# Up projections of a feed-forward by seven products of quarters, with down projections between them

## The chip, the cores and the metric

The kernel runs on one core of a Trainium2 chip. The metric is the device time of one execution in microseconds; lower is better. The kernel before takes 2473.8 us (median of 3 runs, 2471.67 to 2475.36).

## The reference, cut to what matters

Three layers work on 512 tokens of width 1024. Two are hybrid layers with attention, convolution, retention and a feed-forward; the third has a feed-forward, a mixer and a second feed-forward. The change touches the two feed-forwards of the third layer:

```python
def swiglu_ffn(x, w_in, w_down):
    a, b = jnp.split(x @ w_in, 2, axis=-1)
    return (jax.nn.silu(a) * b) @ w_down
...
    x = x + 0.5 * swiglu_ffn(rmsnorm(x, ffn1_norm), ffn1_w_in, ffn1_w_down)
```

`w_in` is 1024 x 5632, so a and b have 2816 columns each, which is 22 blocks of 128; `w_down` is 2816 x 1024. All data are float32.

## The kernel before

Activations lie transposed: 8 tiles of 128 features x 512 tokens. A float32 product is made from three passes of TensorE. Weights and activations are each split into a rounded high part and the rest (`wh`, `wl`; ScalarE copies, VectorE subtracts), and high x high, low x high and high x low are added in PSUM (`mm3`). One output block of an up projection is 8 blocks of k x 3 = 24 matmuls of 128x128 weights against 512 tokens.

`ffn` works in four chunks of 6, 6, 5 and 5 of the 22 blocks (`CH2`). For a chunk it makes the blocks of a and b in turn (`gemm`, `e_up`: times `rb`, the norm's scale for each token; Silu for a; a x b; split into `hid`), and then the eight output blocks of the down projection over this chunk's `hid` (6 or 5 blocks of k x 3 matmuls each), each added to `x` by VectorE (`e_dn`). `wload` loads a weight tile (`raw`, 512 KB) and splits it. The last four down blocks of the second feed-forward run in two halves of 256 tokens (`tail`).

The order of all work is made by a planner. Every call is recorded with its reads and writes (`record`). `order` then gives each engine its list: it steps through an estimated time, starts what can start first, and among those that could start within 20 ns takes the one recorded first. `ahead(n)` makes a piece of work count as recorded n instructions earlier (`AHEAD` = 400 for weights and evictions). `emit` issues everything in the planned order from one line (475), which is why all rows below have that line. Tiles come from pools with a fixed number of buffers: 80 work tiles `t` (`NT`), 3 `raw` (`NR`), 4 `wh` and 4 `wl` (`NW`), 8 PSUM tiles `p` of one bank each (512 float32 a partition).

In `record` an operation depends on those that touched the same columns; and for a tile of a pool, in the order of recording:

```python
op.deps.add(a[-1] if w and eng == "PE" else t[1])
```

`a[-1]` is the last recorded access of this tile, any columns; `t[1]` is the first one. So TensorE's write depends on the last access, all others on the first.

Of the kernel before, what the change touches and what calls it, by code (L numbers as in the profile page):

```python
# [10 lines left out]
F32 = mybir.dt.float32  # L11
F32R = mybir.dt.float32r
AF = mybir.ActivationFunctionType
OP = mybir.AluOpType
AX = mybir.AxisListType

P = 128
S = 512
NB = S // P
D = 1024  # L20
KT = D // P
# [83 lines left out]
CH2 = [(0, 6), (6, 12), (12, 17), (17, 22)]  # L105
FF2 = 22
# [82 lines left out]
class _Engine:  # L189


    def __init__(self, plan, name, real):
        self._plan, self._name, self._real = plan, name, real
# [7 lines left out]
class Plan:  # L201
# [96 lines left out]
    @staticmethod  # L298
    def _cost(eng, method, args, kw, writes, reads):
        out = writes[0]  # L300
        n = 1
        for _, c in out.ap[1:]:
            n *= c

        def psum(x):
            return "PSUM" in str(x.space)

        table = 0
        if eng == "PE":
            if method == "transpose":  # L310
                return 2 * n / 2.4 + 1, 0
            m = reads[0].ap[-1][1] if len(reads[0].ap) == 2 else P
            load = 18 + .695 * m
            if reads[0].dtype == F32:
                return max(4 * n / 2.4, 2 * load) + 3, 0
            return max(n / 2.4, load) + 3, 0
        if eng == "ACT":
            f = kw.get("func", args[2] if len(args) > 2 else None)
            table = Plan.TABLES.get(str(f).split(".")[-1], 0)
            return .833 * n + (51 if psum(reads[0]) else 94) + (187 if "accum_out" in kw else 0), table  # L320
        if eng == "DVE":
            ptr = 60 if n > 8 and any(x.ap[-1][1] == 1 and len(x.ap) == 2 for x in reads) else 0
            if method == "reciprocal":
                return 62 + 8.3 * n, 0
            if method == "tensor_reduce":
                n = 1
                for _, c in reads[0].ap[1:]:
                    n *= c
            fast = method in ("tensor_scalar", "tensor_copy", "memset") and not any(map(psum, writes + reads))
            return 68 + ptr + (.52 if fast else 1.042) * n, 0  # L330
        if eng == "POOL" and method != "dma_start":
            return 80 + (2.3 if method == "tensor_tensor" else 1.28 if method == "affine_select" else 1.0) * n, 0
        b = 4
        for _, c in out.ap:
            b *= c
        run = min(4 * x.ap[-1][1] if x.ap[-1][0] == 1 else 4 for x in writes + reads)
        return b / 360.0 * max(1.0, 512.0 / run), 0


    def order(self):  # L340
# [153 lines left out]
class Net:  # L494
    def __init__(self, ctx, tc, d, where):
        self.tc, self.d, self.where = tc, d, where
        self.nc = self.plan = Plan(tc.nc)
        self.const = ctx.enter_context(tc.tile_pool(name="const", bufs=1))
        self.wp = ctx.enter_context(tc.tile_pool(name="wp", bufs=1))
        self.sb = ctx.enter_context(tc.tile_pool(name="sb", bufs=1))  # L500
        self.dr = ctx.enter_context(tc.tile_pool(name="dr", bufs=1, space=bass.MemoryType.DRAM))
        self.ps = ctx.enter_context(tc.tile_pool(name="ps", bufs=1, space=bass.MemoryType.PSUM))
        self.NT = 80
        self.NR, self.NW = 3, 4
        self.AHEAD = 400
        self.LATER = 300
        self.WAIT = 52
        self.mr = self.px = None
        self.STAT = 40
        self.PARK = 300  # L510
        self.ORDER = "card"
        self.PC, self.PA, self.PR = 4, 1, 1
        self.SHIFT = 10
        self.EARLY = 60
# [142 lines left out]
    def gemm(self, srcs, acts, evict, wide=4, bg=None, steps=0, per=1, both=False):  # L657


        n = len(acts)  # L660
        i = 0
        first = True
        while i < len(srcs):
            g = srcs[i:i + (wide if first else 1)]
            first = False
            with self.plan.ahead(self.AHEAD):
                ws = [self.wload(s, n * P * per) for s in g]
            pss = [[self.psg() for _ in range(per)] for _ in g]
            for k in range(n):
                for (h, l), pp in zip(ws, pss):  # L670
                    for j, ps in enumerate(pp):
                        s = slice((j * n + k) * P, (j * n + k + 1) * P)
                        self.mm3(ps, (h[:, s], l[:, s]), acts[k], k == 0, k == n - 1)
            with self.plan.ahead(self.AHEAD):
                for j, pp in enumerate(pss):
                    evict(i + j, *pp)
            i += len(g)
            if bg:
                if both:
                    self.pump_all(bg)  # L680
                else:
                    self.pump(bg, steps)


    def rsqrt(self, v, n):
# [1069 lines left out]
                    nc.sync.dma_start(out[k][:, s], x)  # L1755

    def ffn(self, n, h=None, out=None):
        nc, d = self.nc, self.d
        h = h or self.hsplit(self.x, f"ffn{n}_norm_2")
        with self.plan.ahead(-self.STAT):  # L1760
            rb = self.rms_r(self.x)
        wi, wd = d[f"f{n}_in"], d[f"f{n}_down"]
        at = 0
        for c, (lo, hi) in enumerate(CH2):
            hid = []
            gate = []

            def e_up(i, ps):
                t = self.T()
                nc.vector.tensor_tensor(t, ps, rb, op=OP.mult)  # L1770
                if i % 2 == 0:
                    nc.scalar.activation(t, t, AF.Silu)
                    gate.append(t)
                else:
                    nc.vector.tensor_tensor(t, t, gate.pop(), op=OP.mult)
                    hid.append(self.split(t))

            srcs = [wi[i + s * FF2] for i in range(lo, hi) for s in range(2)]
            self.gemm(srcs, h, e_up, 4 if c == 0 else 1)

            def e_dn(i, ps):
                nc.vector.scalar_tensor_tensor(self.x[i], ps, 0.5, self.x[i], op0=OP.mult, op1=OP.add)

            m = P * (hi - lo) * P
            down = [wd[at + i * m:at + (i + 1) * m].rearrange("(p f) -> p f", p=P) for i in range(KT)]
            if out is None or hi < FF2:
                self.gemm(down, hid, e_dn, 1)
            else:
                self.gemm(down[:KT - TAIL], hid, e_dn, 1)
                self.tail(down[KT - TAIL:], hid, out)  # L1790
            at += KT * m
# [164 lines left out]
```

## Time and profile before

| | |
|---|---|
| runs | 2473.8, 2471.67, 2475.36 us |
| profiled execution | 2473.95 us, span 2472.2 us |
| instructions | 30175, of them 11506 matmuls |
| mean granted clock of TensorE | 0.993 |
| HBM read, written | 244.54 MB, 22.04 MB |

The span runs from the first to the last instruction. TensorE's matmuls are shown as PE, its weight loads as PEld, VectorE as DVE, ScalarE as ACT, GpSimd as POOL and SyncE, which issues most transfers, as SP. Matmuls are pipelined, so the duration of one is longer than the distance from its start to the next one's. In the first feed-forward of the third layer the chunks follow each other from about 1258.5 to 1617.6 us, up projections and down projections in turn; the second one runs from about 2120 us to the end.

### The profile page before, as it was taken

The numbers are of one execution on the slowest core, as the hardware profiler recorded it, in microseconds if no ns is written. First come the engines' busy times: TensorE is split into PE (matmuls) and PEld (weight loads), VectorE is DVE, ScalarE is ACT, GpSimd is POOL, SyncE is SP. The second block draws the span as 40 slices with busy tenths as digits, with TensorE's granted clock in tenths as the row PEclk, the third lists the DMA queues.
The fourth block names the chain that finished last, engine by engine and source line by source line (L and its number), as shares of the span: only waits on it lengthen the run. The fifth ranks groups of instructions, "written<-read, shape, count | busy, mean of one in ns | idle before, by whom it ended". The sixth has DMA issues, their size and how long they took to land. (4 is left out here: it accounts for less than half of the span.)

```text
span 2472.2 us, 30175 instructions
## 1 busy us (share of the span) xinstructions
PE 2430.0 (98%) x11506; PEld 2017.0 (82%) x11506; DVE 1464.3 (59%) x2529; ACT 949.2 (38%) x1487; POOL 115.2 (5%) x222
## 2 busy tenths in 40 slices
PE   8999999999998999999999999999999999999998
PEld 7878888888887788788888888888888888888887
DVE  7986834545997689744574444556445455444445
ACT  4467422223347643242342222333455334322222
POOL 0011000000001102300000000000000000000000
PEclk9999999999999999999999999999999999999999
DMA  6552333324454334453323233375222243232232
GB/s 211 160 139 95 112 95 101 96 94 129 135 155 122 117 105 148 136 180 94 119 80 96 90 104 98 102 245 164 90 79 70 75 138 109 84 111 88 90 108 67
DMA packets 104785, 286.12 MB, mean 116 GB/s; under 512 B 14272, under 2 KB 21120, under 8 KB 104640
## 3 DMA queue, kind: packets, MB, share of 16 engines
q1 hardware_dynamic: 99808, 270.79, 35.7%
q0 software_dynamic: 4832, 13.41, 1.8%
q8 instruction: 90, 1.47, 0.2%
q14 instruction: 55, 0.45, 0.1%
HBM read 244.54 MB, written 22.04 MB: 108 GB/s over the span
## 5 line engine op out<-in xcount | busy, mean ns | idle before, releaser
L475 PE MATMUL p<-t,wh 128*128 128x512 f32 (+1 forms) x6408 | 1995.6, 390 | 12.7 <-ACT wh L475 7.5
L475 PEld LDWEIGHTS p<-t,wh 128*128 128x128 f32 x6408 | 1203.7, 189 | 261.6 <-ACT wh L475 9.3
L475 PE MATMUL p<-t,wl 128*128 128x512 f32 x3204 | 1249.7, 390 | 1.2 <-DVE wl L475 1.1
L475 ACT ACTIVATE wh<-raw 128x1024 fp32r<-128x1024 f32 (+4 forms) x428 | 426.1, 1000 | 1181.8 <-PE p L475 790.5
L475 PEld LDWEIGHTS p<-t,wl 128*128 128x128 f32 x3204 | 604.2, 189 | 125.4 <-DVE wl L475 3.6
L475 DVE TENSOR_TENSOR wl<-raw,wh 128x1024 fp32r<-128x1024 f32 (+4 forms) x428 | 491.3, 1151 | 146.7 <-ACT wh L475 142.4
L475 DVE TENSOR_TENSOR t<-p,t 128x512 f32<-128x512 f32 (+5 forms) x388 | 237.0, 629 | 449.3 <-PE p L475 441.0
L475 DVE TENSOR_TENSOR t<-t 128x512 f32<-128x512 f32 (+9 forms) x688 | 361.5, 552 | 45.8 <-ACT t L475 35.7
L475 ACT ACTIVATE t<-t 128x512 f32<-128x512 f32 (+3 forms) x409 | 246.9, 617 | 147.0 <-DVE t L475 129.0
L475 PE MATMUL p<-t 128*128 128x256 f32 (+10 forms) x1184 | 181.5, 294 | 11.9 <-DVE t L475 9.2
L475 PEld LDWEIGHTS p<-t 128*128 128x128 f32 (+2 forms) x1184 | 148.9, 173 | 38.8 <-DVE t L475 15.7
L475 DVE TENSOR_TENSOR t<-t,p 128x512 f32<-128x512 f32 x104 | 71.7, 692 | 173.6 <-PE p L475 169.3
L475 ACT ACTIVATE t<-p 128x512 f32<-128x512 f32 (+7 forms) x290 | 129.9, 500 | 75.6 <-PE p L475 67.6
L475 DVE SCALAR_TENSOR_TENSOR t<-t,cols 128x512 fp32r<-128x512 f32 (+32 forms) x196 | 133.9, 717 | 8.8 <-ACT t L475 8.7
L475 DVE SCALAR_TENSOR_TENSOR t<-p,t 128x512 f32<-128x512 f32 (+1 forms) x84 | 57.5, 684 | 125.2 <-PE p L475 125.2
L475 ACT ACTIVATE t<-t,cols 128x512 fp32r<-128x512 f32 (+2 forms) x76 | 49.5, 671 | 29.4 <-DVE t L475 28.7
L475 PE MATMUL p<-ident,t 128*128 128x128 f32 x388 | 55.1, 278 | 5.0 <-DVE t L475 2.7
L475 ACT ACT_TABLE_LOAD x42 | 53.9, 1283 | 11.8 <-DMA t<-in_x 4.0
L475 PEld LDWEIGHTS p<-ident,t 128*128 128x128 f32 x388 | 45.8, 142 | 12.8 <-DVE t L475 4.0
L475 ACT ACTIVATE t<-t,s 128x128 f32<-128x128 f32 (+2 forms) x80 | 42.3, 531 | 15.2 <-DVE s L475 14.6
L475 DVE SCALAR_TENSOR_TENSOR t<-t 128x512 f32<-128x512 f32 (+1 forms) x72 | 44.9, 631 | 1.5
L475 DVE CUSTOM_DVE_ANT_0 t<-p,t 128x256 f32<-128x256 f32 (+2 forms) x80 | 34.5, 450 | 9.4 <-PE p L475 9.1
(58 smaller groups left out, 366.2 us busy)
## 6 DMA issues: line engine op xcount, KB each, us to landing
raw<-in_w_in SPq DMA_DIRECT2D x100, 512.0 KB, 3.8
raw<-in_f_in SPq DMA_DIRECT2D x88, 512.0 KB, 3.5
raw<-in_w_up SPq DMA_DIRECT2D x64, 512.0 KB, 3.6
raw<-in_w_down SPq DMA_DIRECT2D x64, 512.0 KB, 3.6
t<-t SPq DMA_DIRECT2D x126, 128.0 KB, 3.3
raw<-in_w_out SPq DMA_DIRECT2D x24, 512.0 KB, 3.6
raw<-in_f_down SPq DMA_DIRECT2D x32, 384.0 KB, 3.0
raw<-in_f_down SPq DMA_DIRECT2D x32, 320.0 KB, 2.8
```

The costliest lines, as they stand in the source:

```text
L475: fn(*args, **kw)
```

## The change

From the second chunk on, the two up blocks of one index i (a's and b's weights, 1024 x 128 each) are computed together. The weights of both are seen as a 2 x 2 matrix of quarters (block a or b; lower or upper half of k), the activations as 2 x 2 quarters (half of k; half of the tokens), and the product of the two is made by seven products of quarters and sums in place of eight products.

- `halves7` makes the sums of activation quarters once for a feed-forward, beside the first chunk, and splits them: 16 work tiles that stay.
- `wload7` makes the sums of weight quarters: four loads from SP, two loads from GpSimd that add to what is there (`accum_op`), two sums on VectorE; three tiles are split as `wh` and `wl`, and one sum (s4) in work tiles.
- `prod7` is one product: 4 blocks of k x 3 matmuls of 256 columns.
- `pair7` runs the seven products into three half banks: a and b are the halves of one PSUM tile, c is in another. Between products ScalarE copies a (`p1`) and VectorE makes `p1 + b` (`u2_`), a times `rb`, and `w`; after them come the last sums.
- The down projections of a chunk are no longer run behind its up projections but kept (`later`) and recorded one by one between and within the pairs of the next chunk. Only the last chunk's run behind its ups.
- Work tiles go from 80 to 74, `raw` from 3 to 4, `wh` and `wl` from 4 to 5 each, in the whole kernel; the planner counts an adding transfer twice.

```diff
--- before.py
+++ after.py
@@ -334,7 +334,7 @@
         for _, c in out.ap:
             b *= c
         run = min(4 * x.ap[-1][1] if x.ap[-1][0] == 1 else 4 for x in writes + reads)
-        return b / 360.0 * max(1.0, 512.0 / run), 0
+        return b / 360.0 * max(1.0, 512.0 / run) * (2 if kw.get("accum_op") else 1), 0
 
 
     def order(self):
@@ -500,8 +500,8 @@
         self.sb = ctx.enter_context(tc.tile_pool(name="sb", bufs=1))
         self.dr = ctx.enter_context(tc.tile_pool(name="dr", bufs=1, space=bass.MemoryType.DRAM))
         self.ps = ctx.enter_context(tc.tile_pool(name="ps", bufs=1, space=bass.MemoryType.PSUM))
-        self.NT = 80
-        self.NR, self.NW = 3, 4
+        self.NT = 74
+        self.NR, self.NW = 4, 5
         self.AHEAD = 400
         self.LATER = 300
         self.WAIT = 52
@@ -680,6 +680,104 @@
                     self.pump_all(bg)
                 else:
                     self.pump(bg, steps)
+
+
+    def halves7(self, gname):
+
+
+        nc, C = self.nc, S // 2
+        V = nc.vector
+        lo, hi = slice(0, C), slice(C, S)
+        out = []
+        for k in range(KT // 2):
+            a, b = self.T(), self.T()
+            nc.scalar.activation(a, self.x[k], AF.Copy, scale=self.col(gname, k))
+            nc.scalar.activation(b, self.x[k + KT // 2], AF.Copy, scale=self.col(gname, k + KT // 2))
+            q1, q2 = self.T(), self.T()
+            V.tensor_tensor(q1[:, lo], a[:, lo], a[:, hi], op=OP.subtract)
+            V.scalar_tensor_tensor(q1[:, hi], q1[:, lo], -1.0, b[:, hi], op0=OP.mult, op1=OP.subtract)
+            V.tensor_tensor(q2[:, lo], b[:, hi], a[:, hi], op=OP.subtract)
+            V.scalar_tensor_tensor(q2[:, hi], q1[:, hi], -1.0, b[:, lo], op0=OP.mult, op1=OP.subtract)
+            out.append((self.split(q1), self.split(q2)))
+            yield out
+
+    def wload7(self, u1, u2):
+
+        nc = self.nc
+        V = nc.vector
+        n = KT * P
+        lo, hi = slice(0, n // 2), slice(n // 2, n)
+        r1, r2, r3 = (self.plan.pool_tile(self.wp, (P, n), F32, "raw", self.NR) for _ in range(3))
+        nc.sync.dma_start(r1, u1)
+        nc.sync.dma_start(r2[:, lo], u2[:, lo])
+        nc.sync.dma_start(r3[:, lo], u2[:, hi])
+        nc.sync.dma_start(r3[:, hi], u1[:, lo])
+        nc.gpsimd.dma_start(r2[:, lo], u2[:, hi], accum_op=OP.add)
+        nc.gpsimd.dma_start(r3[:, hi], u2[:, lo], accum_op=OP.add)
+        s4 = self.T()
+        V.tensor_tensor(r2[:, hi], r2[:, lo], r1[:, lo], op=OP.add)
+        V.tensor_tensor(s4, r2[:, hi], r1[:, hi], op=OP.add)
+        out = []
+        for r in (r1, r2, r3):
+            h = self.plan.pool_tile(self.wp, (P, n), F32R, "wh", self.NW)
+            l = self.plan.pool_tile(self.wp, (P, n), F32R, "wl", self.NW)
+            nc.scalar.activation(h, r, AF.Copy)
+            V.tensor_tensor(l, r, h.bitcast(F32), op=OP.subtract)
+            out.append(((h[:, lo], l[:, lo]), (h[:, hi], l[:, hi])))
+        (a11, a12), (s1, s2), (a22, s3) = out
+        return a11, a12, a22, s1, s2, s3, self.split(s4)
+
+    def prod7(self, o, w, acts, start):
+
+        mm = self.nc.tensor.matmul
+        wh, wl = w
+        n = len(acts)
+        for k, (ah, al) in enumerate(acts):
+            c = slice(k * P, (k + 1) * P)
+            mm(o, wh[:, c], ah, start=start and k == 0, stop=False, skip_group_check=True)
+            mm(o, wl[:, c], ah, start=False, stop=False, skip_group_check=True)
+            mm(o, wh[:, c], al, start=False, stop=(k == n - 1), skip_group_check=True)
+
+    def pair7(self, u1, u2, h, q):
+
+
+
+        nc, C, K = self.nc, S // 2, KT // 2
+        V = nc.vector
+        lo, hi = slice(0, C), slice(C, S)
+
+        def part(ts, c):
+            return [(x[:, c], y[:, c]) for x, y in ts]
+
+        with self.plan.ahead(self.AHEAD):
+            a11, a12, a22, s1, s2, s3, s4 = self.wload7(u1, u2)
+        q1, q2 = [x for x, _ in q], [y for _, y in q]
+        ab, c = self.psg(), self.psg()[:, lo]
+        a, b = ab[:, lo], ab[:, hi]
+        self.prod7(a, a11, part(h[:K], lo), True)
+        self.prod7(b, s2, part(q1, hi), False)
+        self.prod7(c, s1, part(q1, lo), True)
+        t = self.T()
+        p1, u2_ = t[:, lo], t[:, hi]
+        with self.plan.ahead(self.AHEAD):
+            nc.scalar.activation(p1, a, AF.Copy)
+        self.prod7(a, a12, part(h[K:], lo), False)
+        with self.plan.ahead(self.AHEAD):
+            V.tensor_tensor(u2_, p1, b, op=OP.add)
+        self.prod7(b, s3, part(q2, lo), False)
+        yield None
+        o1, o2 = self.T(), self.T()
+        w = self.T(F32, (P, C))
+        with self.plan.ahead(self.AHEAD):
+            yield a, o1
+            V.tensor_tensor(w, p1, b, op=OP.add)
+            V.tensor_tensor(o2[:, hi], w, c, op=OP.add)
+        self.prod7(b, a22, part(q2, hi), False)
+        self.prod7(c, s4, part(h[K:], hi), False)
+        with self.plan.ahead(self.AHEAD):
+            V.tensor_tensor(o2[:, lo], p1, b, op=OP.add)
+            V.tensor_tensor(o1[:, hi], u2_, c, op=OP.add)
+            yield o1, o2
 
 
     def rsqrt(self, v, n):
@@ -1755,35 +1853,73 @@
                     nc.sync.dma_start(out[k][:, s], x)
 
     def ffn(self, n, h=None, out=None):
+
+
         nc, d = self.nc, self.d
+        V = nc.vector
         h = h or self.hsplit(self.x, f"ffn{n}_norm_2")
         with self.plan.ahead(-self.STAT):
             rb = self.rms_r(self.x)
         wi, wd = d[f"f{n}_in"], d[f"f{n}_down"]
+        C = S // 2
+        lo, hi = slice(0, C), slice(C, S)
         at = 0
-        for c, (lo, hi) in enumerate(CH2):
+        q = []
+
+        def sums():
+            for o in self.halves7(f"ffn{n}_norm_2"):
+                q[:] = o
+                yield
+
+        bg = [sums()]
+        later = []
+        for c, (c0, c1) in enumerate(CH2):
             hid = []
             gate = []
 
             def e_up(i, ps):
                 t = self.T()
-                nc.vector.tensor_tensor(t, ps, rb, op=OP.mult)
+                V.tensor_tensor(t, ps, rb, op=OP.mult)
                 if i % 2 == 0:
                     nc.scalar.activation(t, t, AF.Silu)
                     gate.append(t)
                 else:
-                    nc.vector.tensor_tensor(t, t, gate.pop(), op=OP.mult)
+                    V.tensor_tensor(t, t, gate.pop(), op=OP.mult)
                     hid.append(self.split(t))
 
-            srcs = [wi[i + s * FF2] for i in range(lo, hi) for s in range(2)]
-            self.gemm(srcs, h, e_up, 4 if c == 0 else 1)
+            if c == 0:
+                srcs = [wi[i + s * FF2] for i in range(c0, c1) for s in range(2)]
+                self.gemm(srcs, h, e_up, 4, bg, 1)
+                self.finish(bg)
+            else:
+                m = 2 * (c1 - c0)
+                at_ = [-(-i * KT // m) for i in range(m + 1)]
+                for j in range(c1 - c0):
+                    g = self.pair7(wi[c0 + j], wi[c0 + j + FF2], h, q)
+                    next(g)
+                    for f in later[at_[2 * j]:at_[2 * j + 1]]:
+                        f()
+                    a, o1 = next(g)
+                    V.tensor_tensor(o1[:, lo], a, rb[:, lo], op=OP.mult)
+                    o1, o2 = next(g)
+                    V.tensor_tensor(o1[:, hi], o1[:, hi], rb[:, hi], op=OP.mult)
+                    nc.scalar.activation(o1, o1, AF.Silu)
+                    V.scalar_tensor_tensor(o2, o2, -1.0, rb, op0=OP.mult, op1=OP.mult)
+                    V.tensor_tensor(o2, o2, o1, op=OP.mult)
+                    hid.append(self.split(o2))
+                    next(g, None)
+                    for f in later[at_[2 * j + 1]:at_[2 * j + 2]]:
+                        f()
 
             def e_dn(i, ps):
-                nc.vector.scalar_tensor_tensor(self.x[i], ps, 0.5, self.x[i], op0=OP.mult, op1=OP.add)
-
-            m = P * (hi - lo) * P
+                V.scalar_tensor_tensor(self.x[i], ps, 0.5, self.x[i], op0=OP.mult, op1=OP.add)
+
+            m = P * (c1 - c0) * P
             down = [wd[at + i * m:at + (i + 1) * m].rearrange("(p f) -> p f", p=P) for i in range(KT)]
-            if out is None or hi < FF2:
+            if c1 < FF2:
+                later = [lambda i=i, hid=hid, down=down: self.gemm([down[i]], hid, lambda _, ps: e_dn(i, ps), 1)
+                         for i in range(KT)]
+            elif out is None:
                 self.gemm(down, hid, e_dn, 1)
             else:
                 self.gemm(down[:KT - TAIL], hid, e_dn, 1)
```

## Rows read from the trace of the kernel before

**Rows 1.** The page, busy us of each engine, share of the span, instructions.

```profile
PE 2430.0 (98%) x11506; PEld 2017.0 (82%) x11506; DVE 1464.3 (59%) x2529; ACT 949.2 (38%) x1487; POOL 115.2 (5%) x222
```

**Rows 2.** The page, 40 slices: granted clock in tenths, and GB/s moved.

```profile
PEclk9999999999999999999999999999999999999999
...
GB/s 211 160 139 95 112 95 101 96 94 129 135 155 122 117 105 148 136 180 94 119 80 96 90 104 98 102 245 164 90 79 70 75 138 109 84 111 88 90 108 67
```

**Rows 3.** Stretches: downs of chunk 0, ups of chunk 1. Columns as in the first line.

```profile
core 0: us, PE busy (x) PEld busy (x) DVE busy (x) ACT busy (x) POOL busy (x), PEclk, DMA share, GB/s
...
1323.80:1356.50 32.70, 32.70 (x145) 27.05 (x145) 15.23 (x19) 8.08 (x10) 0.00 (x0) 1.00 0.37 110
1356.50:1421.80 65.30, 65.30 (x290) 54.07 (x289) 28.24 (x35) 18.37 (x23) 0.00 (x0) 1.00 0.29 90
```

**Rows 4.** What TensorE waited for: us in total, times, longest.

```profile
PE p L475 <- DVE t L475: 12.3, 18, 2.5
PE p L475 <- ACT wh L475: 7.5, 1, 7.5
PE p L475 <- ACT t L475: 6.3, 6, 2.6
```

**Rows 5.** Timeline of TensorE, last down projections: start us, us, what.

```profile
2434.90 0.39 PE L475 MATMUL p<-t,wl 128*128 128x512 f32 x1
...
2445.10 0.39 PE L475 MATMUL p<-t,wl 128*128 128x512 f32 x1
...
2446.03 0.28 PE L475 MATMUL p<-t,wl 128*128 128x256 f32 x1
...
2452.51 0.28 PE L475 MATMUL p<-t,wl 128*128 128x256 f32 x1
```

**Rows 6.** Groups by form, TensorE: busy us, mean ns | idle before.

```profile
L475 PE MATMUL p<-t,wh 128*128 128x512 f32 x6328 | 1980.8, 392 | 12.7 <-ACT wh L475 7.5 <-ACT t L475 2.6 <-DVE s L475 2.5
...
L475 PE MATMUL p<-t,wh 128*128 128x256 f32 x80 | 14.9, 285 | 0.0
```

**Rows 7.** Groups by form, VectorE and then ScalarE.

```profile
L475 DVE TENSOR_TENSOR wl<-raw,wh 128x1024 fp32r<-128x1024 f32 x348 | 425.5, 1227 | 133.3 <-ACT wh L475 132.1
L475 DVE TENSOR_TENSOR t<-t 128x512 f32<-128x512 f32 x262 | 188.4, 729 | 17.5 <-ACT t L475 8.4 <-POOL t L475 2.6 <-ACT wh L475 0.5
...
L475 DVE TENSOR_TENSOR t<-p,t 128x256 f32<-128x256 f32 x8 | 3.4, 420 | 2.5 <-PE p L475 2.5
...
L475 ACT ACTIVATE wh<-raw 128x1024 fp32r<-128x1024 f32 x348 | 366.9, 1060 | 973.2 <-PE p L475 636.1 <-issue 309.9 <-DMA raw<-in_w_in 12.9
L475 ACT ACTIVATE t<-t 128x512 f32<-128x512 f32 x192 | 120.4, 641 | 11.0 <-DMA t<-sM 6.0 <-DVE t L475 2.9 <-DMA t<-t 1.8
...
L475 ACT ACTIVATE t<-p 128x256 f32<-128x256 f32 x33 | 10.2, 390 | 6.2 <-PE p L475 6.1
```

**Rows 8.** Transfers by issue: count, KB each, us to landing.

```profile
sW<-t POOLq DMA_DIRECT2D x8, 256.0 KB, 3.3
...
raw<-in_mem_up SPq DMA_DIRECT2D x8, 256.0 KB, 2.7
...
t<-su POOLq DMA_DIRECT2D x4, 256.0 KB, 7.7
```

**Rows 9.** Timeline of SP: the first weights of chunk 1 asked for.

```profile
1333.91 0.33 SPq L475 DMA_DIRECT2D raw<-in_f_in  x1
```

**Rows 10.** Timeline in the dilated attention: VectorE reads PSUM, TensorE goes on.

```profile
1737.80 0.40 DVE L475 CUSTOM_DVE_ANT_0 t<-p,t 128x256 f32<-128x256 f32 x1
...
1738.14 0.07 DVE L475 DVE_READ_ACCUMULATOR2_ANT t<- 128x1 f32 x1
...
1738.26 0.40 PEld L475 LDWEIGHTS p<-t 128*128 128x128 f32 x2
```

**Rows 11.** Timeline near the end: VectorE, TensorE and VectorE hand over.

```profile
2464.19 0.16 DVE L475 SCALAR_TENSOR_TENSOR s<-s 128x2 f32<-128x2 f32 x1
...
2464.40 0.69 PE L475 MATMUL p<-ident,s 128*128 128x128 f32 x2 [1.60 <-DVE s L475]
2465.13 0.48 DVE L475 SCALAR_TENSOR_TENSOR t<-t,cols,p 128x256 f32<-128x256 f32 x1 [0.78 <-PE p L475]
```

## The prediction

> **What bounds the kernel now.** I read the first two parts of the page first. [...] Busy matmul time alone doesn't show that TensorE is the limit, so the next view is the table of stretches inside the first feed-forward. In the eight down projections of chunk 0, and in the six pairs of up projections of chunk 1 behind them, TensorE is busy for the whole stretch at a clock of 1.00; VectorE works for less than half of it, GpSimd not at all, the DMA engines for about a third [rows 3]. TensorE's waits say the same from the other side: over the whole kernel it waits 12.3 us for VectorE's tiles, 6.3 us for ScalarE's, and 7.5 us once for weights [rows 4]. So time here is the number of matmuls times their pitch, and a wait put into that stream is paid in full.
>
> **The change part by part.** There are 6 + 5 + 5 pairs in chunks 1 to 3 of one feed-forward, 32 in both.
>
> *Fewer columns.* The pitch is read from starts in a dense stretch. Matmuls of 512 columns: 2434.90 to 2445.10 is 45 of them, 226.7 ns each. Of 256 columns, with new weights for each: 2446.03 to 2452.51 is 54, 120.0 ns each [rows 5]. The durations beside them, 392 and 285 ns, are longer, because matmuls overlap; the 80 matmuls of 256 columns with high parts of weights, with 40 of low parts between them, are the last projections of the kernel, in the same order of parts as the new products [rows 6]. A pair now is 2 x 8 x 3 = 48 matmuls of 512 columns, 10.88 us; the window agrees, 65.3 / 6 [rows 3]. With the change it is 7 x 4 x 3 = 84 of 256, 10.08 us. That is 0.80 us a pair and 25.7 us in all; an eighth less arithmetic is worth 7.4%, not 12.5%, because the half-length matmul costs 53% of the long one.
>
> [...]
>
> *VectorE and ScalarE.* A pair brings three subtractions of weights at 1.227 us, six operations on 512 columns at about 0.72, seven on 256 at 0.42: 10.9 us. ScalarE gets three conversions at 1.06, one copy from PSUM at 0.39 and three passes at 0.64: 5.5 us [rows 7]. In chunk 1 that is 6 x 10.9 + 15.2 for the downs [rows 3] = 81 us of VectorE beside 6 x 10.08 + 32.7 = 93 us of TensorE: 87% counted with full durations, which overlap a little. It fits only because the downs lie between the pairs; the pairs alone would ask for 10.9 beside 10.08. Cost nothing, with TensorE as cover; without that cover it is 0.8 us a pair. The sums of activations (4 x 2.7 us ScalarE, 4 x 3.1 us VectorE) go beside chunk 0's ups, whose first four weights alone are 32 x 3 x 0.227 = 22 us of TensorE: nothing.
>
> *Transfers.* For a pair SP issues four loads where it issued two, GpSimd two adding ones that wait for two of SP's. Nothing else is queued behind them on GpSimd in this stage [rows 3]. Bytes go from 1.0 to 1.75 MB a pair; with the downs' share that is about 2.3 MB in 15.5 us, 145 GB/s, under the 245 GB/s that the kernel moves in one slice [rows 2]. A half load lands in 2.7 us, a 256 KB transfer from GpSimd in 3.3 to 7.7 [rows 8]; one that adds isn't in the trace. I take 4 us, near the plain ones. Chunk 1's first weights are now asked for at 1333.91 [rows 9] and used from 1356.5, 22 us ahead; with three tiles to a pair and one raw buffer more I estimate half of that, so it is hidden; if one landed 4 us late, VectorE's queue would stop at the sum that needs it, and the evictions behind it too.
>
> *Buffers.* One more raw, one more converted weight, six fewer work tiles, in all stages. TensorE's three largest waits sum to 26 us in the whole kernel, 7.5 of it one wait for weights [rows 4]. At best half of that one goes, at worst the waits for work tiles grow by half: between -4 and +9 us. I take 0, since no row shows that work tiles run short.
>
> *Two halves in one bank.* This is the part I hold to decide it. In `pair7` the products a and b share one PSUM tile. ScalarE's copy of a is wanted as soon as the first product ends, and by then the second product is writing b; VectorE's eviction of a (times rb) is wanted when a's second product ends, while s3 writes b. The planner delays a TensorE write for the last recorded access of its tile, but a read only for the first access and for writers of its own columns. So it places both reads a fifth of a microsecond into the other half's product, some two matmuls in. What the kernel does where two engines use one bank can be seen in the dilated attention: VectorE reads the first half of a tile from 1737.80, its accumulator is read until 1738.21, and only at 1738.26 does TensorE load weights for the second half's scores [rows 10]. If the program keeps this order also between the planned places, the read waits for the matmuls planned ahead of it, and the remaining ten wait for the read.
>
> [...]
>
> The price: the last matmul ahead of the read takes 0.28 from its start [rows 6], the hop to the reader 0.04, from the reader back to TensorE 0.05 [rows 11], the read 0.39 on ScalarE or 0.42 on VectorE [rows 7]; less the pitch of 0.12 it is 0.64 and 0.67 us, 1.31 a pair, 41.9 us over 32 pairs. It lies near the mean of TensorE's present waits for VectorE, 12.3 / 18 = 0.68 us. A third read (p1 + b) has s1's 1.4 us as cover, and meets a's next product only where VectorE is more than a microsecond late: perhaps one pair in ten, 2 us. The third sum (w) is waited for by plan; a down or the next pair stands in front.
>
> **Sum.** The profiled execution took 2473.95 us (span 2472.2), 0.15 above the median shown, which I neglect. 2473.95 - 25.7 + 41.9 + 2 = 2492.
>
> **Rivals.**
> 1. *Both reads hold TensorE* (forecast): 2492; its own range is 2480 to 2504, by the unknown buffers and the price per wait. For it: the order of the plan and the handshake of [rows 10]. Against: the handshake there is one that the planner itself asked for. Chance 0.53.
> 2. *The other sign: no hold.* The reads run beside the other half's product, or fall behind it, because ScalarE and VectorE are late enough. Then only the pitch counts: 2473.95 - 25.7 + 2 = 2450. It decides where waits cost under 23.7 / 32 = 0.74 us a pair, about one of the two. For it: VectorE is busy up to 87% of the time, so a read may start late; but a product lasts 1.44 us and the longest operation in front 1.2. Chance 0.28.
> 3. *One of the two holds*: 2450 + 21 = 2471, no change. Chance 0.07.
> 4. *VectorE's queue becomes the bound*, by an adding transfer that lands late or by its 87%: a microsecond or more a pair on top of case 1, 2492 + 16 to 32, above 2508. For it: TensorE would now wait for VectorE in the middle of products. Against: the 10 us of lead. Chance 0.09.
> 5. *A short matmul costs half a long one*, 113.3 ns in place of 120, with both holds: 84 x 6.7 ns x 32 = 18 us less than case 1, 2474, no change. Against: 54 matmuls in a row at 120.0. Chance 0.03. [...]
>
> **Numbers.** About 0.2%, 5 us, is what a measurement of this kernel tells from no change. Slower by more: cases 1 and 4, 0.62. Within it: 3 and 5, 0.10. Faster: case 2, 0.28. The predicted time is that of case 1. The range goes from the lower side of case 2, 2446, to 2514, which leaves out most of case 4 and little else; both signs lie in it, and the likeliest's own range is above.
>
> **What would show each step.** Pitch: 256-column matmuls on wh and wl start 120 ns apart inside a product. Hold: TensorE's waits for ScalarE's and VectorE's t grow from 18.6 us to about 60, with some 64 more of them, 0.6 to 0.7 us each, behind a copy from PSUM of 256 columns and behind a product with rb of 256; in the stretches of chunks 1 to 3 the matmuls do not follow without gaps. No hold: those waits stay near 20 us, and chunk 1's ups and chunk 0's downs together shrink from 98 us [rows 3] to 93. Transfers: if GpSimd's adding loads land later than 5 us, VectorE's sums of raw wait for DMA. Buffers: a difference ahead of the first feed-forward, by the time at which its first weights are issued. I am wrong if the reads run through without stopping TensorE, or if the transfers, not the bank, hold it.

## The result, and the profile after

| | runs | median us | range | against before, 95% interval |
|---|---|---|---|---|
| before | 4 | 2472.74 | 2471.64 to 2475.36 | |
| after | 4 | 2493.06 | 2491.26 to 2495.22 | 1.0081 [1.0064, 1.0098] |

The kernel became 20 us slower. The profiled execution took 2493.18 us (span 2491.4). Lines of its page: the busy time of each engine, the granted clock by slices, and the adding loads (count, KB each, us to landing):

```profile
PE 2417.2 (97%) x12658; PEld 2052.1 (82%) x12658; DVE 1633.2 (66%) x2897; ACT 1029.9 (41%) x1614; POOL 170.6 (7%) x286
...
PEclk9999999999999999999999999999999999999999
...
raw<-in_f_in POOLq DMA_DIRECT2D x64, 256.0 KB, 4.3
```

TensorE is busy for 13 us less than in [rows 1], and yet the span is 19 us longer. The clock isn't the cause: it stays in the top digit, as in [rows 2]. What TensorE waited for (total, times, longest) against [rows 4]:

```profile
PE p L475 <- DVE t L475: 30.2, 51, 1.7
PE p L475 <- ACT t L475: 19.4, 39, 0.9
PE p L475 <- ACT wh L475: 10.4, 5, 8.8
```

The two upper rows together went from 18.6 to 49.6 us, and from 24 waits to 90. Where they lie is seen in the timeline of one pair in the first feed-forward (start, duration, engine, in brackets the idle time ahead and what ended it):

```profile
1345.48 0.28 PE L475 MATMUL p<-t,wl 128*128 128x256 f32 x1
1345.86 0.38 ACT L475 ACTIVATE t<-p 128x256 f32<-128x256 f32 x1 [0.46 <-PE p L475]
...
1346.30 0.50 PE L475 MATMUL p<-t,wh 128*128 128x256 f32 x2 [0.53 <-ACT t L475]
...
1346.64 0.28 PE L475 MATMUL p<-t,wl 128*128 128x256 f32 x1
...
1347.50 0.42 DVE L475 TENSOR_TENSOR t<-t,p 128x256 f32<-128x256 f32 x1 [0.70 <-PE p L475]
...
1351.06 0.40 PE L475 MATMUL p<-t,wh 128*128 128x256 f32 x2
1351.50 0.42 DVE L475 TENSOR_TENSOR t<-p,t 128x256 f32<-128x256 f32 x1 [0.27 <-PE p L475]
...
1351.98 0.39 PE L475 MATMUL p<-t,wl 128*128 128x256 f32 x1 [0.52 <-DVE t L475]
```

ScalarE's copy `p1` begins after the matmul of 1345.48 has ended, and TensorE goes on at 1346.30, released by ScalarE: 0.82 us from start to start where 0.12 is the pitch. The product with `rb` does the same at 1351.50. The read at 1347.50 (`u2_`, also from the shared tile) stops nothing: TensorE is then in s1, which has a bank of its own. Counted in matmuls of the pair, 25 of the 31 copies stop TensorE behind the second matmul of s2 (this one behind the fifth), and 22 of the 29 products with `rb` behind the tenth of s3.

From the starts of all matmuls in both feed-forwards, everything beyond the pitch (0.227 and 0.120 us) was summed. Before, there was no such gap over 0.4 us in the same stages; after, there are these:

```
gap over 0.4 us beyond the pitch, by the read that lies in it   count   sum us   median us
  ScalarE's copy p1                                               31      20.0      0.63
  VectorE's product with rb                                       29      19.6      0.68
  VectorE's sum p1 + b                                             4       3.5      0.67
short gaps, 64 of them on the next matmul behind one of these     66       7.1      0.10
all                                                                       50.2
```

The short gaps are visible above, too: the two matmuls from 1346.30 take 0.34 us until the next start at 1346.64, where two pitches are 0.24.

### The profile page after: what moved, and what is told of

Read it like the earlier page. It is cut to its first block, busy times and chain, and to the rows that moved or that the text cites. A ratio compares the mean times of both kernels' runs of the same rounds, so it can differ in the third digit from the quotient of the medians.

```text
span 2491.4 us, 33366 instructions
## 1 busy us (share of the span) xinstructions
PE 2417.2 (97%) x12658; PEld 2052.1 (82%) x12658; DVE 1633.2 (66%) x2897; ACT 1029.9 (41%) x1614; POOL 170.6 (7%) x286
## 4 chain that ended last, share of the span: by engine, by line
PE 87%; DVE 6%; DMA 2%; ACT 2%; issue 2%; SPq 1%; POOL 0%; DVEq 0%; ACTq 0%; POOLq 0%
PE p L475 87%; DVE t L475 5%; ACT t L475 2%; DVE wl L475 1%; DMA t<-t 1%; DMA raw<-in_f_in 1%; SPq L475 1%; ACT wh L475 0%; POOL t L475 0%; DMA raw<-in_w_in 0%; DMA t<-sW 0%; DVE s L475 0%; DMA t<-in_x 0%; DMA sW<-t 0%; DMA t<-sM 0%
## 5 line engine op out<-in xcount | busy, mean ns | idle before, releaser
L475 PE MATMUL p<-t,wl 128*128 128x512 f32 (+1 forms) x3460 | 1267.3, 366 | 14.4 <-DVE t L475 14.0
L475 ACT ACTIVATE wh<-raw 128x1024 fp32r<-128x1024 f32 (+2 forms) x460 | 458.8, 1004 | 1003.7 <-PE p L475 781.1
L475 DVE TENSOR_TENSOR wl<-raw,wh 128x1024 fp32r<-128x1024 f32 (+2 forms) x460 | 527.3, 1151 | 162.2 <-ACT wh L475 159.6
L475 ACT ACTIVATE t<-t 128x512 fp32r<-128x512 f32 (+6 forms) x457 | 277.6, 619 | 218.2 <-DVE t L475 199.8
L475 DVE TENSOR_TENSOR t<-p,t 128x512 f32<-128x512 f32 (+6 forms) x356 | 205.9, 599 | 246.7 <-PE p L475 236.7
L475 DVE TENSOR_TENSOR t<-t,p 128x256 f32<-128x256 f32 (+1 forms) x264 | 137.9, 525 | 193.6 <-PE p L475 187.0
L475 PE MATMUL p<-t 128*128 128x256 f32 (+9 forms) x1568 | 233.7, 292 | 14.2 <-DVE t L475 7.5
L475 ACT ACTIVATE t<-p 128x512 f32<-128x512 f32 (+8 forms) x322 | 141.8, 488 | 122.6 <-PE p L475 116.2
L475 POOL DMA_DIRECT2D raw<-in_f_in x64 | 54.5, 851 | 849.5 <-DVE t L475 489.4
L475 DVE SCALAR_TENSOR_TENSOR t<-t 128x512 f32<-128x512 f32 (+2 forms) x120 | 73.5, 617 | 2.0
L475 ACT ACT_TABLE_LOAD x41 | 52.6, 1283 | 15.2 <-PE p L475 6.3
```

The costliest lines, as they stand in the source:

```text
L475: fn(*args, **kw)
```

## The experiments

Each ratio is against runs of the kernel before on the same chip: its median was 2474.37 us (14 runs) for the first four kernels and 2474.6 us (13 runs) for the last four. By these ratios the changed kernel's 1.0081 is about 2494 us there.

| kernel | median us | runs | ratio to before, 95% interval |
|---|---|---|---|
| `three_banks` | 2444.48 | 4 | 0.9873 [0.9856, 0.9889] |
| `a_with_c` | 2446.61 | 4 | 0.9881 [0.9866, 0.9896] |
| `reads_wait` | 2470.72 | 10 | 0.9985 [0.9967, 1.0003] |
| `buffers_only` | 2467.83 | 5 | 0.9971 [0.9956, 0.9986] |
| `copy_waits` | 2474.62 | 10 | 1.0004 [0.9992, 1.0016] |
| `pair_reads_wait` | 2445.8 | 4 | 0.9891 [0.9875, 0.9908] |
| `plain_loads` | 2444.49 | 4 | 0.9878 [0.9863, 0.9892] |
| `downs_first` | 2447.28 | 4 | 0.9891 [0.9876, 0.9906] |

**`three_banks`: a, b and c each in a bank of its own**

```diff
-        ab, c = self.psg(), self.psg()[:, lo]
-        a, b = ab[:, lo], ab[:, hi]
+        a, b, c = (self.psg()[:, lo] for _ in range(3))
...
-        self.prod7(b, s2, part(q1, hi), False)
+        self.prod7(b, s2, part(q1, hi), True)
```

> The changed kernel with a, b and c in three PSUM banks of their own instead of a and b in one. If the shared bank is what holds TensorE (my theory): the 64 long holds of 0.65 to 0.69 us and the 64 short ones of 0.10 behind them, 50.3 us in the two feed-forwards, go, and the time is 2493 - 50 = 2443 us, 1.2% under the kernel before. Rival, VectorE's or the transfers' lateness holds it wherever the reads lie: the holds stay with other neighbours, 2485 to 2493 us. Second rival, three banks a pair make PSUM scarce: new waits in front of first products, 2450 to 2470 us.

Measured: 2444.48 us, 49 us less than the changed kernel, and faster than the kernel before as well. No gap over 0.4 us is left in the feed-forwards (from 1300 to 1620 us the trace has no wait of TensorE), and the waits are near the level of [rows 4] again. TensorE's waits:

```profile
PE p L475 <- DVE t L475: 14.7, 18, 2.1
PE p L475 <- ACT wh L475: 9.3, 5, 7.7
PE p L475 <- ACT t L475: 4.4, 9, 0.9
```

The same copy of a in the timeline of this kernel:

```profile
1343.53 0.40 PE L475 MATMUL p<-t,wh 128*128 128x256 f32 x2
1343.59 0.37 ACT L475 ACTIVATE t<-p 128x256 f32<-128x256 f32 x1
...
1343.77 0.28 PE L475 MATMUL p<-t,wl 128*128 128x256 f32 x1
```

The copy runs from 1343.59 to 1343.96 while TensorE starts a matmul every 0.12 us. Nothing else was changed, so the shared bank cost the whole loss and more.

**`a_with_c`: the shared bank holds a and c instead of a and b**

```diff
-        ab, c = self.psg(), self.psg()[:, lo]
-        a, b = ab[:, lo], ab[:, hi]
+        ac, b = self.psg(), self.psg()[:, lo]
+        a, c = ac[:, lo], ac[:, hi]
```

(The first product into b then has `start` set, and the first into c no longer does.)

> The changed kernel with a and c as the halves of one bank and b in another: still two banks a pair, and still one bank shared by two products. My theory says that only the neighbour counts: a is read while TensorE writes b, so the holds go as with three banks, 2443 us. Rival, any sharing of a bank costs: about 64 holds stay, 2485 to 2495 us. Rival, the lateness of VectorE or the transfers: no change, 2493 us.

Measured: 2446.61 us, with no gap over 0.4 us left in the feed-forwards. TensorE's waits:

```profile
PE p L475 <- DVE t L475: 14.2, 16, 1.8
...
PE p L475 <- ACT t L475: 3.8, 7, 0.9
```

The number of PSUM tiles is that of the changed kernel, so it isn't the third tile that helps in `three_banks`. What counts is which two accumulators share a bank: while a is read, TensorE is now in s2 or s3, which write b elsewhere.

**`reads_wait`: every read of a PSUM tile is planned behind the tile's last recorded access, in the whole kernel**

```diff
-                        op.deps.add(a[-1] if w and eng == "PE" else t[1])
+                        op.deps.add(a[-1] if t[0] == "p" or w and eng == "PE" else t[1])
```

> The changed kernel with a and b in one bank as before, but the planner lets a read of a PSUM tile wait for the last recorded access of that tile, as it does for TensorE's writes. My theory: the holds come from the planned place of the two reads, so with the copy of a behind the second product (beside s1) and a's eviction behind s3, few holds stay: 2443 to 2455 us. The rival that the bank itself is slow when shared, or that VectorE is late: 2480 us or more.

Measured: 2470.72 us, a miss in the time: neither the theory's range nor the rival's. Its ten runs lie between 2463 and 2480 us, the slower ones at a lower granted clock (0.987 against 0.994). In the feed-forwards the gaps fell to 3.6 us, as expected, but ahead of the first feed-forward TensorE lost 23 us against the same matmuls of the kernel with the rule for the pairs alone (below): 9 us of it lay before 868 us, 15 between 992 and 1090 us, and a little came back later. Two stretches of 20 us there, of this kernel:

```profile
core 0: us, PE busy (x) PEld busy (x) DVE busy (x) ACT busy (x) POOL busy (x), PEclk, DMA share, GB/s
1040.00:1060.00 20.00, 10.25 (x44) 7.51 (x43) 7.78 (x10) 2.72 (x6) 5.53 (x10) 0.80 0.16 51
1060.00:1080.00 20.00, 16.88 (x76) 12.62 (x77) 17.23 (x22) 6.97 (x7) 4.58 (x8) 0.77 0.53 155
```

TensorE is busy for 10.25 of the first 20 us, and its granted clock is 0.80 in them and 0.77 in the next 20 us. Most of its waiting in these 40 us is for VectorE:

```profile
PE p L475 <- DVE t L475: 9.7, 3, 4.2
```

A rule that is right for the pairs delays reads elsewhere that were better early. How much of the loss is the waits and how much the lower clock, no run takes apart.

**`pair_reads_wait`: the same rule for the tile of a and b alone**

```diff
-                        op.deps.add(a[-1] if w and eng == "PE" else t[1])
+                        op.deps.add(a[-1] if n in self.whole or w and eng == "PE" else t[1])
...
         a, b = ab[:, lo], ab[:, hi]
+        self.plan.whole.add(ab.tensor.name)
```

> As the changed kernel, but every read of the tile that a and b share is recorded as depending on its last recorded access; all other tiles keep the old rule. Theory (a planned read in the middle of the other half's product is what stops TensorE, and the loss of the rule for all tiles lay outside the feed-forwards): the holds go and nothing else changes, 2493 - 50 = 2443 us, up to 2449. Rival 1 (reads that wait for the whole other product make the evictions and the next pair late): gaps of another kind in the feed-forwards, above 2455. Rival 2 (the loss with the rule for all tiles lay in the pairs after all): 2465 to 2471.

Measured: 2445.8 us; one gap over 0.4 us is left (1.05 us, behind p1 + b). TensorE's waits, and its rows in the stretches shown above, where it is some 9 us ahead of `reads_wait` in its work:

```profile
PE p L476 <- DVE t L476: 15.7, 19, 2.1
...
PE p L476 <- ACT t L476: 4.3, 8, 0.9
```

```profile
1040.00:1060.00 20.00, 16.58 (x71) 12.36 (x70) 15.13 (x18) 7.00 (x10) 1.08 (x2) 1.00 0.53 182
1060.00:1080.00 20.00, 18.52 (x101) 14.61 (x102) 14.12 (x20) 11.56 (x15) 7.81 (x14) 1.00 0.82 267
```

So a read that waits for the whole other product (12 matmuls, 1.4 us) costs nothing here, while one that is planned inside it stops TensorE. The bank may stay shared if the plan knows of it. The loss of `reads_wait` lay elsewhere.

**`copy_waits`: the rule for the copy p1 alone**

```diff
+            self.plan.whole.add(ab.tensor.name)
             nc.scalar.activation(p1, a, AF.Copy)
+            self.plan.whole.clear()
```

> As the changed kernel, but only ScalarE's copy of a (p1) is recorded as depending on the last access of the shared tile; the product with rb keeps its place in s3. Theory (two independent holds a pair, each 0.65 to 0.69 us and 0.10 of the next matmul): 32 of the 64 holds go, 32 x 0.79 = 25 us less, 2468 us, and 32 long gaps stay, all behind VectorE. Rival (the holds are not independent, the copy only meets the next product instead): 64 gaps stay, 2485 or more.

Measured: 2474.62 us, 19 us less than the changed kernel by the ratios where 25 were expected, between the theory and its rival. The copy's gaps are all gone, and the 29 behind the product with rb stay at 19.7 us. But p1 + b now stops TensorE nine times (8.1 us) where it did four times (3.5 us). One of the nine, VectorE and TensorE alone:

```profile
1326.48 0.42 DVE L476 TENSOR_TENSOR t<-t,p 128x256 f32<-128x256 f32 x1 [0.65 <-PE p L476]
...
1326.96 0.50 PE L476 MATMUL p<-t,wh 128*128 128x256 f32 x2 [0.58 <-DVE t L476]
```

All gaps sum to 32.0 us, 18 less than after: the time follows the gaps. The holds are priced one by one, but they aren't independent: some of the sums p1 + b now meet a's next product. In six of the nine, as in the one shown, the copy had ended 1.1 to 1.6 us before, and VectorE waited for the matmul that the plan has ahead of the sum; that the later copy moved the sum there in the plan is likely, but no run shows it. In the other three, the longest, VectorE was late by a sum of raw that had waited for a transfer.

**`buffers_only`: the kernel before with the changed numbers of buffers**

```diff
-        self.NT = 80
-        self.NR, self.NW = 3, 4
+        self.NT = 74
+        self.NR, self.NW = 4, 5
```

> The kernel before with only the numbers of buffers changed: 74 work tiles, 4 raw, 5 high and 5 low weight tiles. The pitch gives -25.7 and the holds +50.3 us, 24.6, and the spans differ by 19.2; the trace after gains 3.6 us in the second mixer, where only buffers differ. If that is the buffers: 2473 - 4 to 5 = 2468 us. If the difference comes from the interleaving, or from one profiled run: 2473 us.

Measured: 2467.83 us, 0.9971 of before, as expected. The profiled span is 2466.1 against 2472.2 us. By the starts of the same matmuls its lead is 2.8 us at some 1017 us, 0.9 from 1100 us to the end of the first feed-forward, 5.0 from 1800 us (in the mixer) and 6.0 at the end.

**`plain_loads`: `three_banks` without the adding**

```diff
-        nc.gpsimd.dma_start(r2[:, lo], u2[:, hi], accum_op=OP.add)
-        nc.gpsimd.dma_start(r3[:, hi], u2[:, lo], accum_op=OP.add)
+        nc.gpsimd.dma_start(r2[:, lo], u2[:, hi])
+        nc.gpsimd.dma_start(r3[:, hi], u2[:, lo])
```

> The version with a bank for each of a, b and c, whose two adding loads of a pair are plain loads that overwrite; left out are the two sums of weight quarters that these loads make. The planner's cost for them stays doubled, so the order of work is the same. Theory (the adding loads land far ahead of their use): no difference, 2444 within 3 us, though the loads themselves land in about 3.5 us in place of 4.3. Rival (they cost TensorE waits for weights or bandwidth): 2436 or less.

Measured: 2444.49 us, no difference. The loads land in 3.2 us (4.5 in `three_banks`) and their issue occupies GpSimd for 539 ns instead of 853. The group of these issues on GpSimd (busy time, mean ns, idle time ahead by releaser), here and in `three_banks`:

```profile
L476 POOL DMA_DIRECT2D raw<-in_f_in x64 | 34.5, 539 | 825.5 <-DVE t L476 577.9 <-DMA raw<-in_f_in 217.5 <-DVE wl L476 13.7
```

```profile
L475 POOL DMA_DIRECT2D raw<-in_f_in x64 | 54.6, 853 | 807.2 <-DVE t L475 525.7 <-DMA raw<-in_f_in 193.1 <-DVE wl L475 61.2
```

The same transfers among the DMA issues of its page (count, KB each, us to landing):

```profile
raw<-in_f_in POOLq DMA_DIRECT2D x64, 256.0 KB, 3.2
```

**`downs_first`: `three_banks` with the down projections ahead of the pairs**

```diff
+                for f in later:
+                    f()
+                later = []
                 for j in range(c1 - c0):
```

> The version with a bank for each of a, b and c, but the down projections of the chunk ahead are recorded before the first pair instead of between and within the pairs. By the prediction's term (10.9 us of VectorE beside 10.08 of TensorE for a pair) 0.8 us a pair are lost, 32 x 0.8 = 26 us: 2470, with TensorE waiting for VectorE. Rival (operations of VectorE overlap: it was busy 200 us in the stretch of 16 pairs and 24 downs, less 24 x 1.9 for the downs that is 9.6 a pair, under 10.08): it fits without cover, 2445 to 2450.

Measured: 2447.28 us, 3 us over `three_banks`. Three stretches of pairs without downs in its first feed-forward:

```profile
1354.20:1412.00 57.80, 57.80 (x482) 57.61 (x481) 48.83 (x82) 27.94 (x38) 6.82 (x8) 1.00 0.63 160
1447.50:1495.30 47.80, 47.80 (x398) 47.60 (x398) 39.74 (x67) 22.38 (x31) 5.98 (x7) 1.00 0.61 152
1525.40:1573.90 48.50, 48.06 (x398) 47.65 (x397) 41.55 (x70) 22.74 (x32) 5.13 (x6) 1.00 0.67 164
```

VectorE is busy for 130.1 of 154.1 us, 84%, and TensorE for 153.7 of them: the pairs nearly fit without the downs between them. Two gaps over 0.4 us come up in the two feed-forwards, 2.5 us together, where TensorE waits for p1 + b; ahead of the longer one (1.9 us) VectorE had worked for 3 us without a pause.

## Why the prediction was right

Forecast and result agree to 1 us, and the mechanism is the one forecast. That they agree so closely is luck: some terms were off, by up to 7 us, and their errors cancelled:

| term | predicted us | measured us | from |
|---|---|---|---|
| fewer columns | -25.7 | -25.7 | pitch 0.120 and 0.227 |
| two holds a pair | +41.9 | +39.6 | 60 gaps: 31 at 0.65, 29 at 0.68 |
| the third read | +2 | +3.5 | 4 gaps |
| the next matmul behind a hold | 0 | +7.1 | 66 short gaps |
| buffers | 0 | -5 to -6 | all but the feed-forwards; `buffers_only` |
| sum | +18 | +19 | span 2472.2 to 2491.4 |

By the starts of the same matmuls, the changed kernel loses 24.4 us to the kernel before in the two feed-forwards, the sum of the first four rows of the table, and gains 5 us in all else.

*Fewer columns* held: 1281 matmuls of 256 columns in the first feed-forward that follow without a gap are 119.6 ns apart. So the fifth rival's pitch of 113.3 ns is out. With the holds gone, `three_banks` shows what the arithmetic and the buffers are worth: 2474 - 25.7 - 6 = 2442, measured 2444.5.

*The holds* are shown by two versions that move the accumulators to other banks and one that moves only the reads; all three end between 2444 and 2447 us, which is what the second rival (no hold, 2450) would have given, less the buffers' 6. TensorE's waits for `t` grew to 49.6 us where I had said about 60, with 66 more of them where I had said 64. I had added prices counted beyond the pitch of 0.12, but a wait is counted from the end of the row ahead, 0.28 us from its start: the matmul at 1346.30 shows 0.53 us of idle time in a gap of 0.70. The 0.16 us of difference, 64 times, are the missing 10 us. The copies stand some two matmuls into s2, as forecast; the products with `rb` mostly stand ten into s3, and why the plan has them there is open. It makes no difference to the price. That the program keeps the order on both sides is what the timeline shows: ScalarE's copy is released by TensorE (0.46 us of idle time at 1345.86), and TensorE by ScalarE or VectorE (0.53 us at 1346.30, 0.52 at 1351.98), though the columns differ. A read of another bank ran beside matmuls: the copy in `three_banks`, from 1343.59 to 1343.96, with a matmul started every 0.12 us. Every PSUM tile of this kernel has a bank to itself, so the runs don't tell whether the order is kept for the tile or for the bank. Whether the chip could serve both halves of one bank at once was not tried.

*The price of a hold* was right for the gap itself (0.64 and 0.67 predicted) but ended too early: the second matmul behind it also starts 0.10 us late, 0.22 instead of 0.12. Its weight load starts 0.11 us behind the first matmul's start, where in the stream it starts with it. That is the mis-sized term, 7 us.

*The buffers* are the other one. I took 0 in a range of -4 to +9 us; they gave 5 to 6 us less, a little outside it. The argument there looked at TensorE's largest waits alone.

*VectorE* was over-counted. Its cover by the downs was to be worth 0.8 us a pair, 26 us; without it, 3 us were lost. I had counted 81 us of VectorE in the 93 us of chunk 1, 87%. Without holds, in `three_banks`, chunk 1 takes the 93 us foreseen, with TensorE busy throughout, and VectorE is busy for 70 of them, 75%:

```profile
1323.60:1417.00 93.40, 93.40 (x650) 87.36 (x649) 70.17 (x111) 38.65 (x50) 9.90 (x12) 1.00 0.56 146
```

The durations in the trace overlap (in the changed kernel's stretch of 1310 to 1606 us the rows of VectorE sum to 215 us, busy is 200, 67% of the stretch). And in `downs_first` part of the pairs' sums is made ahead, beside the downs: its three stretches have 1278 matmuls, 15.2 pairs, but 36 subtractions of weights of 1024 columns where so many pairs have 46.

*The transfers* were right in what matters: 4.3 us for an adding load against an estimate of 4, and nothing is gained if they don't add. But they aren't as hidden as I said: 15 of the 64 adding loads took over 5 us to land, and VectorE's sums of raw waited for loads eight times, 11.9 us in all. In `three_banks` such waits sum to 14.5 us and stop TensorE nowhere. In the changed kernel two of the four gaps at p1 + b stand behind one, 2.2 us together. This is the fourth rival's path, at a price of two gaps instead of 32. The two groups, changed kernel and `three_banks`, and the longer gap:

```profile
L475 DVE TENSOR_TENSOR raw<-raw 128x512 f32<-128x512 f32 x32 | 21.9, 686 | 12.0 <-DMA raw<-in_f_in 11.9
```

```profile
L475 DVE TENSOR_TENSOR raw<-raw 128x512 f32<-128x512 f32 x32 | 22.1, 690 | 14.8 <-DMA raw<-in_f_in 14.5
```

```profile
1415.39 0.69 DVE L475 TENSOR_TENSOR raw<-raw 128x512 f32<-128x512 f32 x1 [1.72 <-DMA raw<-in_f_in]
...
1417.33 0.41 DVE L475 TENSOR_TENSOR t<-t,p 128x256 f32<-128x256 f32 x1
...
1417.79 0.39 PE L475 MATMUL p<-t,wh 128*128 128x256 f32 x1 [1.43 <-DVE t L475]
```

Left open: why the buffers' lead falls from 2.8 to 0.9 us and rises to 5; no run takes the three sizes apart.

## What to carry to other kernels

Where a program keeps order for a whole PSUM tile of one bank, as here, two accumulators may share it if none of them is read while TensorE writes the other (`a_with_c`, 2446.61 us); where one is, such a read stops TensorE for the read, two hops and a late next matmul, here 0.75 to 0.78 us, and two of them a pair ate more than an eighth less arithmetic gave. Pair accumulators by when they are read, or tell the planner that a read depends on the whole bank, but only for those tiles (`pair_reads_wait`, 2445.8 us, against `reads_wait`, 2470.72). And count a saving in matmuls by the measured pitch of the shorter shape (0.120 us for 256 columns against 0.227 for 512), not by columns.

## What was not expected of the hardware

A 256 KB load that adds took 4.5 us to land and 853 ns of GpSimd for its issue (`three_banks`), against 3.2 us and 539 ns for the same load without adding (`plain_loads`); without adding the kernel took the same time (2444.49 against 2444.48 us). VectorE's rows overlapped, so that their sum overstated its load by 7% (215 against 200 us, changed kernel, 1310 to 1606 us). The second matmul behind each of the 64 long gaps of the changed kernel started 0.22 us after the first, where the pitch is 0.12 us. In `reads_wait`, from 1040 to 1060 us, TensorE was busy for 10.25 of 20 us and its granted clock was 0.80; in the next 20 us it was 0.77.
